# Attention scores of two heads on half of the array's rows each, in place of zero padded keys

## The chip, the cores and the metric

One core of a Trainium2 chip runs the whole program. Its engines are TensorE (PE; its weight loads are listed apart as PEld), VectorE (DVE), ScalarE (ACT), GpSimd (POOL) and SyncE (SP), each with its own instruction stream that it works through in order. The metric is device time in microseconds (us), median of the runs.

## What is computed

The program is two blocks after each other. The change touches the first one, an attention block on 512 tokens of width 1024 with two kinds of heads of 64 channels. In "A", eight query heads share two heads of keys and values, look back over a window of 128 positions and have a sink in the softmax. In "B", eight heads have keys and values of their own and a mask with three dilations. Cut to what matters here:

```
q_a, k_a = rope(rmsnorm(q_a)), rope(rmsnorm(k_a))       # 8 and 2 heads of 64
o_a = softmax with sink(q_a k_a^T / 8 + window mask) v_a
q_b, k_b = rope(rmsnorm(q_b)), rope(rmsnorm(k_b))       # 8 and 8 heads of 64
o_b = dilated softmax(q_b k_b^T / 8) v_b
x = x + concat(o_a * silu(g_a), o_b * silu(g_b)) @ w_out
```

A second block follows (two layers with a convolution, a state space scan and 16 experts); its code is the same before and after.

## The kernel before

The tokens are four blocks of 128. Projections (line 271, function `mm3`) split each fp32 operand in a high and a low part and add three products in PSUM. Queries and keys come out with the token on the partition, `head_norm_rope` (lines 455 to 469) norms and rotates them, and `transposed` (line 538) turns the heads of a pair into a tile with 128 rows: 64 channels of one head above 64 of the other. `qT` is such a tile of queries. For the keys there are four tiles `kz[i][j]`: `i` says in which half of the rows a head's keys stand (the other half is zeros, written once by GpSimd on line 532), `j` alternates between key heads (A) or pairs (B). With the zeros, `qT` with both heads against `kz[n][j]` gives the scores of head n alone, from a matmul over all 128 rows.

`attend` handles one head: four blocks of queries, each with a score matmul (line 552) of `nb * 128` columns into a PSUM bank `ax` (there are three banks of that name), and a DVE instruction that adds the mask, writes the scores to `P` in SBUF and gives the negative of each row's maximum, `negm` (line 555). In A, `nb` is 1, 2, 2, 2; in B, 1, 2, 3, 4. Then come the exponentials with their sums on ACT (line 564), the reciprocal (568) and four scalings on DVE (570). `values` turns the scaled P back with transposes (line 581, also into `ax`), copies them (584 on ACT, 586 on DVE) and multiplies by v (line 589), the two heads of the pair in two halves of the array's columns. There are four pairs in A and four in B.

Nothing in the code fixes how the engines' streams are interleaved: a scheduler orders the instructions of all of block 1 when the program is built. It fills the time of a softmax on TensorE with projections of later stages (line 271), and it mixes on DVE the softmax with splits of weights (256), with `head_norm_rope` of the next stage's queries and keys, and with gates. In `head_norm_rope` DVE makes `hxn` (463), GpSimd reads it in two instructions (466), DVE then overwrites `hxn` (468), which must wait until GpSimd has read it, and adds (469).

## Time and profile before

| | us |
|---|---|
| median of 3 runs (1655.51 to 1656.25) | 1655.83 |
| span of the profiled execution, first to last instruction | 1652.9 |
| PE busy, share of the span | 1431.6 (87%) |
| DVE busy | 1107.1 (67%) |
| ACT busy | 774.2 (47%) |
| POOL busy | 327.0 (20%) |
| mean granted TensorE clock | 0.933 |

The profiled execution's own time isn't listed beside its span; the median lies 2.9 us above the span. The scores stand between 72.8 and 246.9 us, in the first seventh of the program. A timeline row gives the start, the length, the engine, the line and operation, the output and inputs, how many instructions were merged, and in brackets the idle time of the engine before it with what ended it. Each fp32 score matmul leaves two records, as it runs in two parts.

### The profile page before, as it was taken

Reading aid. Unit: us, or ns where it says so; the run is one execution under the profiler, and the core shown is the slowest. Engines: PE = TensorE matmul, PEld = TensorE weight load, DVE = VectorE, ACT = ScalarE, POOL = GpSimd, SP = SyncE. Lnnn points to the kernel's source line nnn. Section 1 sums busy time; section 2 is a strip of 40 time slices with the busy share of each in tenths; the row PEclk is TensorE's granted clock in tenths of the full one; section 3 lists DMA queues with packets and bytes.
Section 4 is the critical chain, followed back from the end, with each engine's and each line's share of the span. In section 5 each row is a group of like instructions: output and inputs, shape, how many; then the busy total and the mean of one; then the engine's idle time right before and its main releaser. Section 6 shows DMA issues by size and latency. Waiting matters only on the chain. (4 is left out here: it accounts for less than half of the span.)

```text
span 1652.9 us, 21781 instructions
## 1 busy us (share of the span) xinstructions
PE 1431.6 (87%) x7746; PEld 1062.8 (64%) x7754; DVE 1107.1 (67%) x2318; ACT 774.2 (47%) x1367; POOL 327.0 (20%) x259
## 2 busy tenths in 40 slices
PE   7989999979999898996776997589999897977882
PEld 5878767858888553664555776268874365755661
DVE  5877555459999655525975675479966455789772
ACT  5444555234532455423554565335425443666651
POOL 1212000000000320001533343000013001359641
PEclk9999999979999999999897999689999899899896
DMA  5111244121213177424787896511215753799853
GB/s 212 52 52 57 77 153 141 64 90 51 64 62 130 60 243 245 140 74 162 242 268 239 244 265 171 186 42 61 77 64 176 232 194 140 239 322 318 296 165 125
DMA packets 74835, 256.07 MB, mean 155 GB/s; under 512 B 10080, under 2 KB 12512, under 8 KB 74592
## 3 DMA queue, kind: packets, MB, share of 16 engines
q1 hardware_dynamic: 64640, 225.77, 39.9%
q0 software_dynamic: 10080, 28.86, 7.3%
q8 instruction: 62, 1.02, 0.3%
q14 instruction: 53, 0.43, 0.1%
HBM read 230.46 MB, written 31.98 MB: 159 GB/s over the span
## 5 line engine op out<-in xcount | busy, mean ns | idle before, releaser
L271 PE MATMUL mm<-act,uhi 128*128 128x512 f32 (+1 forms) x1504 | 324.0, 362 | 4.4 <-ACT act L416 4.1
L271 PEld LDWEIGHTS mm<-act,uhi 128*128 128x128 f32 x1504 | 249.6, 193 | 68.5 <-issue 16.0
L271 PE MATMUL mm<-act,ulo 128*128 128x512 f32 (+1 forms) x752 | 167.7, 358 | 0.0
L271 PEld LDWEIGHTS mm<-act,ulo 128*128 128x128 f32 x752 | 125.8, 193 | 24.3 <-issue 4.6
L255 ACT ACTIVATE uhi<-raw 128x1024 fp32r<-128x1024 f32 x58 | 61.2, 1059 | 112.0 <-PE mm L271 84.2
L806 DVE SCALAR_TENSOR_TENSOR cvx<-vx,pr,cvx 128x456 f32<-128x456 f32 (+18 forms) x176 | 107.8, 616 | 2.3 <-ACT cvx L789 1.2
L1407 PE MATMUL mm<-act,uhi 128*128 128x512 f32 x328 | 96.6, 417 | 14.2 <-ACT uhi L255 14.2
L271 PE MATMUL mm<-whi,act 128*128 128x256 f32 x576 | 84.4, 293 | 10.7 <-ACT whi L255 10.5
L382 PE MATMUL ad<-raw,sc 128*32 128x512 f32 x384 | 87.9, 658 | 4.9 <-DMA raw<-wada 2.8
L1445 POOL DMA_INDIRECT acc<-k,idx x35 | 67.3, 1923 | 117.0 <-ACT k L1442 35.0
L256 DVE TENSOR_TENSOR ulo<-raw,uhi 128x1024 fp32r<-128x1024 f32 x58 | 70.7, 1221 | 24.5 <-ACT uhi L255 9.1
L271 PEld LDWEIGHTS mm<-whi,act 128*128 128x128 f32 x576 | 76.4, 197 | 14.2 <-ACT whi L255 10.5
L256 DVE TENSOR_TENSOR act<-rawm,act 128x1024 fp32r<-128x1024 f32 x52 | 68.2, 1312 | 20.0 <-ACT act L255 17.4
L256 DVE TENSOR_TENSOR part<-rawm,part 128x1024 fp32r<-128x1024 f32 x40 | 57.0, 1427 | 35.4 <-ACT part L255 27.3
L1407 PEld LDWEIGHTS mm<-act,uhi 128*128 128x128 f32 x328 | 61.7, 196 | 27.7 <-ACT uhi L255 15.1
L1394 PE MATMUL ax<-cs,k 128*128 128x128 f32 x280 | 42.4, 298 | 38.0 <-DMA k<-t_d,idx 38.0
L256 DVE TENSOR_TENSOR act<-raw,act 128x1024 fp32r<-128x1024 f32 x51 | 67.3, 1322 | 11.8 <-ACT act L255 11.5
L990 POOL TENSOR_TENSOR xw<-xstc,swgtc 128x512 f32<-128x512 f32 x8 | 9.7, 1232 | 313.8 <-ACT xstc L844 177.0
L1407 PE MATMUL mm<-part,uhi 128*128 128x512 f32 x232 | 67.5, 412 | 3.6 <-ACT uhi L255 3.2
L271 PE MATMUL mm<-act,whi 128*128 128x512 f32 x256 | 69.9, 412 | 0.0
L255 ACT ACTIVATE act<-rawm 128x1024 fp32r<-128x1024 f32 x52 | 55.1, 1059 | 25.7 <-PE mm L1407 16.7
L255 ACT ACTIVATE act<-raw 128x1024 fp32r<-128x1024 f32 x60 | 63.0, 1053 | 8.2 <-DMA raw<-wd 3.7
(497 smaller groups left out, 3058.1 us busy)
## 6 DMA issues: line engine op xcount, KB each, us to landing
raw<-wada SPq DMA_DIRECT2D x96, 512.0 KB, 5.0
raw<-wgu SPq DMA_DIRECT2D x66, 512.0 KB, 6.3
rawm<-wgu SPq DMA_DIRECT2D x62, 512.0 KB, 6.3
raw<-win SPq DMA_DIRECT2D x40, 512.0 KB, 3.7
raw<-wd SPq DMA_DIRECT2D x34, 512.0 KB, 6.1
rawm<-wd SPq DMA_DIRECT2D x30, 512.0 KB, 6.6
raw<-w SPq DMA_DIRECT2D x26, 512.0 KB, 5.2
raw<-wo SPq DMA_DIRECT2D x24, 512.0 KB, 4.8
```

The lines of the kernel that those rows point to most:

```text
L255: self.nc.scalar.activation(hi, raw, AF.Copy)
L256: (eng or self.nc.vector).tensor_sub(lo, raw, hi.bitcast(F32))
L271: nc.tensor.matmul(out, lhsT=(ah, ah, al)[p], rhs=(bh, bl, bh)[p], start=(start and p == 0 and i == 0), stop=(stop and p == 2 and i == n - 1))
L382: nc.tensor.matmul(ps[32 * g:32 * g + 32], lhsT=self.sc[:, 4 * h + g, :], rhs=w[g // 2][:, 512 * (g % 2):512 * (g % 2) + 512], start=(h == ...
L806: nc.vector.scalar_tensor_tensor(o_, v_, cw[:, l, i, k:k + 1], o_, op0=OP.mult, op1=OP.add)
L990: nc.gpsimd.tensor_tensor(hv(xw), hv(s.xst[:, c]), s.wgt[:, c, 8 * d:8 * d + 8, None].to_broadcast([128, 8, 64]), op=OP.mult)
L1394: nc.tensor.transpose(pt[:, 128 * k:128 * k + 128], j.xg[:, 512 * hf + 128 * k:512 * hf + 128 * k + 128], self.ident)
L1407: nc.tensor.matmul(pg, lhsT=(xh, xl, xh)[p][:, 4 * q + k, :], rhs=(wh, wh, wl)[p][k // 2][:, 512 * (k % 2):512 * (k % 2) + 512], start=(n ...
L1445: nc.gpsimd.indirect_dma_start(out=acc[:, :], out_offset=bass.IndirectOffsetOnAxis(ap=j.sid, axis=0), in_=y, in_offset=None, bounds_check= ...
```

## The change

The keys of a pair stand in one tile `kk[j]` of 128 rows, one head in each half, with no zeros. A score matmul takes 64 rows of `qT` and the same 64 rows of `kk`, so head 0 uses the upper half of the array's rows and head 1 the lower half. `attend` now handles a pair: for each block of queries it issues the matmuls of both heads into two `ax` banks and then the two DVE instructions. The softmax of both heads (`softmax`, the same instructions as before) follows when all eight score matmuls of the pair are written in the code. In B the keys of a pair are copied by one instruction of 128 rows instead of two of 64; the four memsets of GpSimd go. The diff also drops comments and the unused constant's branch (`SCP`), which change nothing.

```
-            kz = [[self.tile(pool, f"kz{i}{j}", [128, 512], bufs=1) for j in range(2)] for i in range(2)]
-            for i in range(2):
-                for j in range(2):
-                    nc.gpsimd.memset(kz[i][j][64 * (1 - i):64 * (1 - i) + 64], 0.0)
...
+            kk = [self.tile(pool, f"kk{j}", [128, 512], bufs=1) for j in range(2)]
...
-            def attend(which, h, qT, kT, mask, span):
...
+            def attend(which, pair, qT, kT, mask, span):
...
-                    sc = (self.mm if SCP[which] else self.ax)(nb * 128)
-                    nc.tensor.matmul(sc, lhsT=qT[:, 128 * j:128 * j + 128],
-                                     rhs=kT[:, 128 * (j + 1 - nb):128 * (j + 1)], start=True, stop=True)
...
+                    scs = [self.ax(nb * 128) for _ in range(2)]
+                    for n, sc in enumerate(scs):
+                        nc.tensor.matmul(sc, lhsT=qT[64 * n:64 * n + 64, 128 * j:128 * j + 128],
...
+                    for (h, negm, lsum, P, tiles), sc in zip(heads, scs):
+                        p = tiles[place[j][0]][:, place[j][1]:place[j][1] + nb * 128]
...
-                for i in range(2):
-                    nc.vector.tensor_copy(kz[i][p % 2][64 * i:64 * i + 64], pt[64 * i:64 * i + 64])
+                nc.vector.tensor_copy(kk[p % 2], pt)
...
-                Ps = [attend(1, 2 * p + n, qT, kz[n][p % 2], self.C("maskB"), 4) for n in range(2)]
+                Ps = attend(1, p, qT, kk[p % 2], self.C("maskB"), 4)
```

The scheduler makes a new order of block 1 from this. Behind the block all engines' orders are as before. Two places show what moves. The first is TensorE at the first pair of B; L552 and L551 are the score matmuls, L271 projections, L581 and L585 the transposes of P, in which the number behind the name tells which of the pair's tiles it is. Before:

```order
L552 MATMUL ax_2037<-kz_11_117,qT_2017 128x128
L552 MATMUL ax_2040<-kz_11_117,qT_2017 128x256
L552 MATMUL ax_2043<-kz_11_117,qT_2017 128x384
L552 MATMUL ax_2046<-kz_11_117,qT_2017 128x512
L552 MATMUL ax_2063<-kz_13_119,qT_2017 128x128
L552 MATMUL ax_2066<-kz_13_119,qT_2017 128x256
L271 MATMUL mm_2160<-act_97,whi_2149 128x512
L552 MATMUL ax_2069<-kz_13_119,qT_2017 128x384
L552 MATMUL ax_2072<-kz_13_119,qT_2017 128x512
L271 MATMUL mm_2160<-act_97,whi_2149 128x512
L271 MATMUL mm_2160<-act_99,whi_2149 128x512
L581 MATMUL ax_2084<-cs,P_2034 128x128
```

The same place after:

```order
L551 MATMUL ax_2035<-kk_11_117,qT_2011 128x128
L551 MATMUL ax_2036<-kk_11_117,qT_2011 128x128
L551 MATMUL ax_2041<-kk_11_117,qT_2011 128x256
L551 MATMUL ax_2042<-kk_11_117,qT_2011 128x256
L551 MATMUL ax_2047<-kk_11_117,qT_2011 128x384
L551 MATMUL ax_2048<-kk_11_117,qT_2011 128x384
L551 MATMUL ax_2053<-kk_11_117,qT_2011 128x512
L551 MATMUL ax_2054<-kk_11_117,qT_2011 128x512
L271 MATMUL mm_2153<-act_97,whi_2142 128x512 x2
L271 MATMUL mm_2153<-act_99,whi_2142 128x512 x2
L271 MATMUL mm_2153<-act_94,whi_2142 128x512 x2
L585 MATMUL ax_2077<-cs,P_2027 128x128
```

The eight scores now alternate between the heads and stand in one piece, and six projections stand between them and the first transpose, where four stood around and behind the scores.

The second place is DVE at the fourth pair of A, between the scores' instructions and the first scaling of P. L567 and L571 add the sink to the sums, L568 and L572 are the reciprocals, L570 and L574 the scalings; L463, L468 and L469 are `head_norm_rope` of B's keys, the other rows its rsqrt. Before:

```order
L567 TENSOR_TENSOR lsum_1037<-lsum_1037,es_1052 128x4
L323 TENSOR_SCALAR rsg_1634<-rsg_1634 128x16
L568 RECIPROCAL lsum_1037<-lsum_1037 128x4
L324 TENSOR_SCALAR rsm_1632<-rsm_1632 128x16
L327 TENSOR_TENSOR rsq_1633<-rsg_1634 128x16
L570 TENSOR_SCALAR P_1038<-P_1038,lsum_1037 128x128
```

The same place after:

```order
L330 SCALAR_TENSOR_TENSOR hr_1618<-rsq_1627,hr_1618 128x16
L463 TENSOR_TENSOR hxn_1642<-b_233_1160,hr_1618 128x512
L463 TENSOR_TENSOR hxn_1648<-b_233_1160,hr_1618 128x512
L468 TENSOR_TENSOR hxn_1642<-hxn_1642,tC_1474 128x512
L571 TENSOR_TENSOR lsum_1031<-lsum_1031,es_1062 128x4
L468 TENSOR_TENSOR hxn_1648<-hxn_1648,tC_1474 128x512
L572 RECIPROCAL lsum_1031<-lsum_1031 128x4
L469 TENSOR_TENSOR b_233_1160<-hxn_1642,b_233_1160 128x4x128
L574 TENSOR_SCALAR P_1032<-P_1032,lsum_1031 128x128
```

Two `hxn`, both of their overwritings and one addition have moved ahead of the reciprocal and the scaling. Of the four pairs of A, the first and the third had the two L463, one or two L468 ahead of the first scaling before as well; after, the first, third and fourth have the rows shown here, with L469. On TensorE the projections of 256 columns between a pair's first score and its first transpose number 47, 29, 32 and 25 before, and 58, 30, 41 and 47 after.

## Rows read from the trace of the kernel before

**Rows 1.** Busy time by stretch: TensorE, its weight loads, DVE, ACT, POOL, clock, DMA.

```profile
core 0: us, PE busy (x) PEld busy (x) DVE busy (x) ACT busy (x) POOL busy (x), PEclk, DMA share, GB/s
60.00:335.00 275.00, 266.79 (x1646) 206.75 (x1645) 168.50 (x486) 126.53 (x283) 19.82 (x23) 0.98 0.26 87
```

**Rows 2.** Timeline of TensorE, third pair of A: scores, projections, first transpose.

```profile
110.85 3.44 PE L552 MATMUL ax<-kz,qT 128*128 128x128 f32 x16
113.94 0.70 PE L271 MATMUL mm<-wlo,act 128*128 128x256 f32 x3
...
120.52 0.48 PE L581 MATMUL ax<-cs,P 128*128 128x128 f32 x1 [2.46 <-DVE P L570]
```

**Rows 3.** Timeline of TensorE around the first pair of B.

```profile
174.19 1.11 PE L271 MATMUL mm<-whi,act 128*128 128x256 f32 x8
175.13 1.04 PE L538 MATMUL ax<-cs,b 128*128 128x128 f32 x8
...
177.03 3.12 PE L552 MATMUL ax<-kz,qT 128*128 128x128 f32 x12
179.80 0.59 PE L271 MATMUL mm<-act,whi 128*128 128x512 f32 x1
180.29 1.77 PE L552 MATMUL ax<-kz,qT 128*128 128x384 f32 x4
181.50 1.04 PE L271 MATMUL mm<-act,whi 128*128 128x512 f32 x2
```

**Rows 4.** Timeline of DVE, reading the scores of that pair.

```profile
177.64 0.29 DVE L555 CUSTOM_DVE_ANT_0 P<-ax,cs 128x128 f32<-128x128 f32 x1
...
180.15 0.28 DVE L555 CUSTOM_DVE_ANT_0 P<-ax,cs 128x128 f32<-128x128 f32 x1
...
180.37 0.42 DVE L555 CUSTOM_DVE_ANT_0 P<-ax,cs 128x256 f32<-128x256 f32 x1
180.71 0.08 DVE L555 DVE_READ_ACCUMULATOR2_ANT negm<- 128x1 f32 x1
```

**Rows 5.** Timeline of TensorE, first pair of A: its stall, later values and transposes.

```profile
84.52 0.33 PE L581 MATMUL ax<-cs,P 128*128 128x128 f32 x1 [2.67 <-DVE P L570]
...
89.98 0.66 PE L589 MATMUL op<-PT,kva 128*64 128x128 f32 x8
90.57 0.66 PE L581 MATMUL ax<-cs,P 128*128 128x128 f32 x4
```

**Rows 6.** Timeline of DVE, third pair of A: norm and rope ahead of the scaling.

```profile
115.14 1.29 DVE L463 TENSOR_TENSOR hxn<-b,hr 128x512 f32<-128x512 f32 x2
...
117.77 1.20 DVE L468 TENSOR_TENSOR hxn<-hxn,tC 128x512 f32<-128x512 f32 x1 [0.71 <-POOL b L466]
...
119.58 0.69 DVE L468 TENSOR_TENSOR hxn<-hxn,tC 128x512 f32<-128x512 f32 x1 [0.52 <-POOL b L466]
120.19 1.06 DVE L570 TENSOR_SCALAR P<-P,lsum 128x128 f32<-128x128 f32 x4
...
121.53 0.66 DVE L469 TENSOR_TENSOR b<-hxn,b 128x512 f32<-128x512 f32 x1
```

**Rows 7.** Timeline of POOL beside the softmax of A's first pair.

```profile
80.76 3.61 POOL L466 TENSOR_TENSOR b<-hxn,tS 128x256 f32<-128x256 f32 x4 [10.99 <-DVE lsum L567]
```

**Rows 8.** Timelines, fourth pair of A: scores and first transpose on TensorE.

```profile
131.60 2.48 PE L552 MATMUL ax<-kz,qT 128*128 128x128 f32 x12
...
137.83 0.33 PE L581 MATMUL ax<-cs,P 128*128 128x128 f32 x1
```

**Rows 9.** Timeline of DVE, fourth pair of A: first read of scores, later rows.

```profile
132.02 0.29 DVE L555 CUSTOM_DVE_ANT_0 P<-ax,cs 128x128 f32<-128x128 f32 x1 [1.69 <-PE ax L552]
...
135.83 0.69 DVE L351 TENSOR_TENSOR P<-cs,xr 128x512 f32<-128x512 f32 x1
...
137.50 1.06 DVE L570 TENSOR_SCALAR P<-P,lsum 128x128 f32<-128x128 f32 x4
```

**Rows 10.** Busy time and clock behind the third pair's stall, and in B.

```profile
120.20:127.00 6.80, 6.48 (x27) 5.27 (x27) 4.39 (x16) 0.65 (x2) 0.00 (x0) 0.51 0.00 0
180.00:330.00 150.00, 149.74 (x809) 105.73 (x808) 81.27 (x200) 72.31 (x145) 0.24 (x1) 1.00 0.34 113
```

**Rows 11.** Line 675, the copies of B's keys: count, shortest, median and longest in ns.

```profile
L675 DVE COPY kz<-ax x8: 681/688/695, 176.2 to 240.5; 64x512 f32<-64x512 f32 x8
```

More of the change, by code (lines that the diff above doesn't have):

```diff
@@ L539, in transposed @@
                 return pt
-            def attend(which, h, qT, kT, mask, span):
+            def attend(which, pair, qT, kT, mask, span):
                 W = span * 128
-                negm = self.tile(self.sm, "negm", [128, 4])
-                lsum = self.tile(self.sm, "lsum", [128, 4])
-                P = []
-                tiles = [PT() for _ in range(2 + which)]
+                heads = []
+                for n in range(2):
+                    negm = self.tile(self.sm, "negm", [128, 4])
+                    lsum = self.tile(self.sm, "lsum", [128, 4])
+                    heads.append((2 * pair + n, negm, lsum, [], [PT() for _ in range(2 + which)]))
                 place = ((0, 0), (0, 256), (1, 0), (1, 256)) if which == 0 else ((0, 0), (1, 0), (0, 128), (2, 0))
@@ L550, in attend, with softmax @@
                     nb = min(j + 1, span)
-                    sc = (self.mm if SCP[which] else self.ax)(nb * 128)
-                    nc.tensor.matmul(sc, lhsT=qT[:, 128 * j:128 * j + 128],
-                                     rhs=kT[:, 128 * (j + 1 - nb):128 * (j + 1)], start=True, stop=True)
-                    p = tiles[place[j][0]][:, place[j][1]:place[j][1] + nb * 128]
-                    nc.vector.tensor_tensor_reduce(p, sc, mask[:, W - nb * 128:W], -1.0, 1e30, OP.add, OP.min,
-                                                   negm[:, j:j + 1])
-                    P.append(p)
+                    scs = [self.ax(nb * 128) for _ in range(2)]
+                    for n, sc in enumerate(scs):
+                        nc.tensor.matmul(sc, lhsT=qT[64 * n:64 * n + 64, 128 * j:128 * j + 128],
+                                         rhs=kT[64 * n:64 * n + 64, 128 * (j + 1 - nb):128 * (j + 1)],
+                                         start=True, stop=True)
+                    for (h, negm, lsum, P, tiles), sc in zip(heads, scs):
+                        p = tiles[place[j][0]][:, place[j][1]:place[j][1] + nb * 128]
+                        nc.vector.tensor_tensor_reduce(p, sc, mask[:, W - nb * 128:W], -1.0, 1e30, OP.add, OP.min,
+                                                       negm[:, j:j + 1])
+                        P.append(p)
+                return [softmax(which, h, negm, lsum, P) for h, negm, lsum, P, _ in heads]
+            def softmax(which, h, negm, lsum, P):
                 if which == 0:
@@ L638, in block1 @@
                 for i in range(2):
-                    nc.vector.tensor_copy(kz[i][(i + kv) % 2][64 * i:64 * i + 64], pt[64 * i:64 * i + 64])
+                    nc.vector.tensor_copy(kk[(i + kv) % 2][64 * i:64 * i + 64], pt[64 * i:64 * i + 64])
             for p in range(4):
@@ L643, in block1 @@
                 opair, kv = self.op(), p // 2
-                Ps = [attend(0, 2 * p + n, qT, kz[n][kv], self.C("maskA"), 2) for n in range(2)]
+                Ps = attend(0, p, qT, kk[kv], self.C("maskA"), 2)
                 values(Ps, lambda i: [kva[:, i, 192 + 64 * kv:192 + 64 * kv + 64]] * 2, 2, opair)
```

## The prediction

> **What bounds the kernel now.** First I read the busy times by stretch: from 60 to 335 us, where all scores lie, TensorE is busy 266.8 of 275 us and DVE 168.5 [rows 1]. So TensorE sets the pace of this part, and a microsecond taken from its stream counts in full if no wait takes its place. Then I read its timeline for the gaps. Two large ones lie in A, both ended by DVE's scaling of P: 2.67 us at the first pair [rows 5] and 2.46 us at the third [rows 2]. At the fourth pair the first transpose starts at 137.83, 0.33 us behind the scaling, and without a gap [rows 8, 9]. In B there is none: 149.74 us busy of 150, at full clock [rows 10]. Third, the price of the scores. A pair of A takes TensorE from 110.85 to 113.94, 3.09 us [rows 2]; a pair of B 2.77 and 1.21 us with one projection between, 3.98 us [rows 3]. Four pairs of each are 4 x 3.09 + 4 x 3.98 = 28.3 us, 1.7% of the time.
>
> **Scores on half of the rows.** If the two heads ran wholly side by side, half of that, 14.1 us, would go. What limits this is who empties the banks. Three banks serve eight scores, so the fourth score of a pair waits for the first read by DVE, and the eighth for the fifth. DVE's reads follow each other after 0.22 us for 128 columns and 0.34 us for 256 [rows 4], so 0.46 and 0.58 for 384 and 512 at the same step. A pair of B thus needs 2 x (0.22 + 0.34 + 0.46 + 0.58) = 3.2 us of DVE, hardly less than the 3.98 us that TensorE needs today; the two are near balance already.
>
> The twelve records of 1664 columns (128, 256, 384, 512, 128, 256) took 2.77 us [rows 3], 1.66 ns a column: 0.21 us for 128, 0.64 for 384, 0.85 for 512. The first read starts 0.61 us behind the first score [rows 3, 4], 0.40 behind the end of its columns. The chain of the second, fifth and eighth score in B: second read done at 0.61 + 0.22 + 0.22 = 1.05; fifth score until 1.69, its read from 2.09 to 2.55; eighth score until 3.40. The least, by the sum of reads alone, is 0.61 + 1.58 + 0.85 = 3.04.
>
> Going over to half rows and back is not in this trace for rows, but it is for columns. Eight records of 128 columns of the values' product take 0.59 us, 89.98 to 90.57 [rows 5]. One after another they would take 8 x 0.106 = 0.85, two at a time 0.42; so halves do run together, and a visit costs 0.17 more. I take 0.15 a visit for row halves as well. A pair of B then takes 3.2 to 3.55 us instead of 3.98. I take 0.5 us saved, near the chain, 2.0 us in four pairs.
>
> In A the same chain with a first read after 0.42 us [rows 8, 9] gives 0.42 + 0.44 + 0.43 + 0.40 + 0.34 + 0.43 + 0.15 = 2.6 instead of 3.09. Norm rows stand among DVE's reads there, so I take 0.3 a pair, 1.2 us. Together **-3.2 us**, bounds -1 and -5.5.
>
> **What DVE does ahead of the scaling.** The softmax of head 0 now waits for both heads' reads, and the scheduler put more of the next stage's norm and rotation ahead of P's scaling. Everything queued behind it on DVE waits, and TensorE, in order, waits at the first transpose. The third pair shows the price: from the first `hxn` at 115.14 to the scaling at 120.19 DVE needs 5.05 us, of which little is its own work: both overwritings wait for GpSimd [rows 6]. The addition that has moved ahead as well costs 0.66 us [rows 6].
>
> First pair: GpSimd ends its four instructions at 80.76 + 3.61 = 84.37 [rows 7]. Behind that come the second overwriting (0.69), the addition (0.66), the small reciprocal (0.2) and 0.33 us to the transpose: 86.25 in place of 84.52, 1.73 later. Eleven more projections fill 11 x 0.1175 = 1.3 us (eight take 0.94 [rows 3]). With scores 0.3 shorter, the stall is 2.67 + 1.73 - 1.3 + 0.3 = 3.4 us. Third pair: 2.46 + 0.66 - 9 x 0.1175 + 0.3 = 2.4. Both together, 5.8 in place of 5.1: **+0.7 us**.
>
> Fourth pair: no stall before; the scaling came 5.9 us behind the first score [rows 8, 9]. After, the two `hxn`, GpSimd's four instructions, both overwritings and an addition come first. Reads and L351 end 4.9 us behind the first score today (135.83 + 0.69 - 131.60 [rows 8, 9]); I keep 5.0 for them and the rest of the rsqrt. Then 5.05 + 0.66 + 0.33 gives the first transpose at 11.0. TensorE is there after 2.8 + 47 x 0.1175 = 8.3. **+2.7 us**, between 0 (if the projections last longer) and 4.
>
> Behind the third pair's stall the clock stood at 0.51 for 6.8 us [rows 10], which is the lower of its two levels, 1.2 GHz. Dense work would lose half of that, 3.3 us. A third stall of this size should bring one more such stretch, and part of the values' work there waits anyway: **+2.4 us**, between 0 and 3.4.
>
> **At no cost.** Eight copies of 0.69 us [rows 11] become four that I expect to be as long each, 2.8 us less on DVE; in B it is TensorE that is full [rows 10], so nothing is gained. The four memsets leave GpSimd's stream ahead of any score. If B's transposes must wait for the later softmax, up to the 2.0 us saved there is given back; two more projections at the first pair are there to fill it, so I take nothing, and keep it for the range. Behind block 1 the orders are the same; the rest only shifts.
>
> **The sum.** -3.2 + 0.7 + 2.7 + 2.4 = +2.6 us against the profiled execution, whose span of 1652.9 lies 2.9 under the median: 1655.8 + 2.6 = **1658.4 us**.
>
> **The rivals.**
> 1. The waits are hidden: the fill of 47 and 58 projections covers DVE's longer queue, no further cold stretch comes, and the scores' 3.2 us remain: 1652.6. For it speaks that the scheduler gave most projections to just these pairs; against it that it left 2.67 and 2.46 us where the same rows stood ahead.
> 2. The halves don't run together, so the change doesn't do what it says: each score takes 1.66 ns a column alone, the 3.2 us are not saved, and eight visits at 0.15 add 1.2: 1658.4 + 4.4 = 1662.8, slower. It decides from the point where a pair's two scores start one behind the other's end. The values' column halves speak against it [rows 5].
> 3. The scores really halve: -14.1 us and nothing given back: 1641.7. It needs DVE to read twice as fast as it does or more banks; the reads' pace speaks against it [rows 4].
> 4. Half used rows let the clock fall at every pair of B and A: eight stretches of 3.4 us (half of the one in [rows 10]) at half speed cost 13.6 us: 1672. B's column halves stand in 150 us at 1.00 [rows 10], which speaks against it.
>
> The Trainium skill, "TensorEngine Tiling (Array Packing)", section Theoretical Speedup, gives up to two times for a contraction of 64 or less. By that rule alone the time would be that of rival 3; the trace agrees with it for columns (0.59 in place of 0.85 us) and has no row tile to show it for rows.
>
> **How the numbers follow.** The forecast has 0.66, rival 1 0.17, rival 2 0.09, rival 3 0.03, rival 4 0.05. A measurement of this kernel can tell about 0.2%, 3.3 us, from no change. The forecast at +2.6 lies just inside; its unknown terms (scores -5.5 to -1, fourth pair 0 to 4, clock 0 to 3.4, B's transposes 0 to 2) put 0.30 of its 0.66 above +3.3 and 0.36 within. Rival 1 gives 0.11 to no change and 0.06 to faster. Slower: 0.30 + 0.09 + 0.05 = 0.44; same: 0.36 + 0.11 = 0.47; faster: 0.06 + 0.03 = 0.09. The range reaches from rival 1 with slightly more saved, 1652, past rival 2, 1664; rivals 3 and 4 and the tails stay out.
>
> **What would show it.** Score records of a pair in pairs that start within some ns of each other, and a pair of B's scores in 3.2 to 3.6 us: right on the halves. Gaps of TensorE ended by the scaling of P at the first, third and fourth pair of A, near 3.4, 2.4 and 2.7 us, each followed by clock near 0.5: right on DVE's order. Wrong if the fourth pair has no gap, if gaps appear inside the blocks of scores, or if the clock in B falls under 1.00. Block 1's end, some 335 us in, should move by as much as the whole.

## The result, and the profile after

The changed kernel took 1667.55 us (median of 10 runs, 1662.1 to 1672.4) beside 1655.67 for the kernel before on the same chip: by the medians 11.9 us slower, a ratio of 1.0072. The ratio on record, given with its interval, is a little smaller, 1.0062 (95%: 1.0042 to 1.0081). On two other chips the same two kernels gave 1.0066 and 1.0069 on record. The prediction had slower by 2.6 us, 1658.4, and a range that ended at 1664.

The page of the changed kernel, its span and its busy times:

```profile
span 1666.9 us, 21782 instructions
...
PE 1440.2 (86%) x7746; PEld 1062.1 (64%) x7754; DVE 1101.2 (66%) x2314; ACT 774.5 (46%) x1367; POOL 322.4 (19%) x255
```

The stretch that answers to [rows 1], with the same columns:

```profile
60.00:335.00 275.00, 261.55 (x1616) 198.53 (x1615) 164.18 (x482) 124.32 (x280) 17.91 (x20) 0.97 0.26 87
```

TensorE is busy 261.6 us of 275 where it was busy 266.8. It issues the same 2000 records up to L342 (below), waits more, and ends them later. I follow three marks in both traces: the start of L342, which ends block 1 on TensorE; the first projection (L271) behind it; and the end.

| profiled execution, us | before | after | more |
|---|---|---|---|
| start of L342 | 335.6 | 343.0 | 7.4 |
| from there to the first L271 | 18.8 | 22.5 | 3.7 |
| from there to the end of the span | 1298.5 | 1301.4 | 2.9 |

The first two make 11.1 of the 11.9 us by which the medians differ. The third is less than what two executions of one program differ by in that part (further down), so nothing is read into it. The first moves from execution to execution as well: three profiles with TensorE's order of before have L342 at 335.2 to 337.9, five with the changed order have it at 339.9 to 344.5.

**The blocks of scores.** TensorE and then DVE (every other kind of read left out) at the first pair of B, which answers to [rows 3] and [rows 4]:

```profile
181.19 3.76 PE L551 MATMUL ax<-kk,qT 64*128 64x128 f32 x16
184.89 1.43 PE L271 MATMUL mm<-act,whi 128*128 128x512 f32 x5
```

```profile
181.70 0.29 DVE L556 CUSTOM_DVE_ANT_0 P<-ax,cs 128x128 f32<-128x128 f32 x1 [0.66 <-PE ax L551]
...
182.79 0.42 DVE L556 CUSTOM_DVE_ANT_0 P<-ax,cs 128x256 f32<-128x256 f32 x1 [0.22 <-PE ax L551]
...
184.44 0.69 DVE L556 CUSTOM_DVE_ANT_0 P<-ax,cs 128x512 f32<-128x512 f32 x1 [0.18 <-PE ax L551]
```

The block holds TensorE from 181.19 to 184.89, 3.70 us in place of 3.98. The first two scores start 6 ns apart. No later pair does: the two of 256 columns start 0.55 us apart, those of 384 0.36, those of 512 0.56, since from the fourth score on each waits until DVE has emptied a bank. Then DVE waits for them (0.22 and 0.18 us in the rows). A pass of 512 columns here takes 0.53 us to the next on its half. Taken as the time from each score record to TensorE's next record, the eight blocks of the program take 28.1 us after and 27.4 before; only the first pair of A and the first two of B are shorter, by 0.1 to 0.3.

This measure is too kind to full rows. Behind their last pass the projection's record starts 0.03 us later, while the pass still runs; it lasts 0.80 us, the next one 0.40. The same place before:

```profile
181.47 0.59 PE L552 MATMUL ax<-kz,qT 128*128 128x512 f32 x1
181.50 0.80 PE L271 MATMUL mm<-act,whi 128*128 128x512 f32 x1
182.14 0.40 PE L271 MATMUL mm<-act,whi 128*128 128x512 f32 x1
```

With half rows the next record starts 0.52 us behind the last pass. From a pair's first score to the next pair's, with the same instructions on TensorE in between, the first two pairs of B take 21.70 and 19.69 us before, 21.15 and 18.77 after: 0.55 and 0.92 less. For the other pairs the projections in between differ; there only a measure over the whole block compares (below).

**The stalls of A.** The three first transposes that waited for P's scaling (first and third pair, then the fourth with its scores), beside [rows 5], [rows 2] and [rows 8]:

```profile
86.24 0.33 PE L585 MATMUL ax<-cs,P 128*128 128x128 f32 x1 [2.97 <-DVE P L574]
```

```profile
123.49 0.33 PE L585 MATMUL ax<-cs,P 128*128 128x128 f32 x1 [2.39 <-DVE P L574]
```

```profile
133.45 3.22 PE L551 MATMUL ax<-kk,qT 64*128 64x128 f32 x16
...
144.70 0.42 PE L585 MATMUL ax<-cs,P 128*128 128x128 f32 x1 [2.30 <-DVE P L574]
```

They are 0.3 longer, 0.1 shorter and 2.3 new. Behind the third and the new one the clock (the number ahead of the last two) is 0.75 over 6.8 us: half of each stretch at 1.2 GHz, half at 2.4. Before, the third pair had 0.51 over the whole 6.8 [rows 10].

```profile
123.50:130.30 6.80, 6.80 (x41) 5.41 (x41) 4.20 (x15) 2.60 (x6) 0.00 (x0) 0.75 0.00 0
144.70:151.50 6.80, 6.80 (x38) 5.52 (x40) 4.80 (x14) 2.44 (x4) 0.00 (x0) 0.75 0.00 0
```

**New waits behind B's last pair.** TensorE:

```profile
260.73 1.09 PE L593 MATMUL op<-PT,b 128*64 128x128 f32 x14
261.75 1.92 PE L382 MATMUL ad<-raw,sc 128*32 128x512 f32 x16
264.93 1.05 PE L388 MATMUL ad<-cs,P 128*128 128x2 f32 x8 [1.26 <-ACT P L385]
265.92 1.07 PE L302 MATMUL ax<-P,cs 128*32 128x256 f32 x6
268.08 2.50 PE L271 MATMUL mm<-act,whi 128*128 128x512 f32 x5 [1.10 <-ACT whi L255]
```

The last adaLN step of block 1 (L382, L388) now stands alone behind the values, without a projection in its pauses. With another wait of 0.27 that ends at 228.83 this makes 2.6 us, where B had none [rows 10].

**The join of block 1 and the next part.** TensorE again:

```profile
342.97 1.05 PE L342 MATMUL ax<-cs,P 128*128 128x1 f32 x8 [0.69 <-ACT P L305]
347.25 2.08 PE L355 MATMUL ax<-P,cs 128*128 128x512 f32 x2 [3.22 <-DVE P L351]
358.82 3.64 PE L382 MATMUL ad<-raw,sc 128*32 128x512 f32 x16 [9.50 <-DVE P L415]
363.27 1.87 PE L388 MATMUL ad<-cs,xw 128*128 128x2 f32 x8 [0.80 <-ACT xw L385]
365.48 0.79 PE L271 MATMUL mm<-act,uhi 128*128 128x256 f32 x2 [0.34 <-ACT uhi L255]
```

Before, L382 ran right behind L355, from 341.84 on, and the long wait (7.17 us) stood behind it at L388. After, L382 itself waits for the last of the L415, where DVE reads the norm's factor that L355 wrote. The order of instructions is the same; the bank is not. The factor is a tile `ax` of block 1 and lies in bank 0, and bank 0 is `ad` in the next part, by the banks that the two programs assign. In the kernel before, the rotation of the three `ax` banks had put it in bank 2. No trace shows these numbers; that the bank is the cause is tested below (e1_join).

**The 7.4 us up to L342.** TensorE has 2000 records up to there in both programs:

```profile
0.00:335.55 335.55, 315.63 (x2000) 249.50 (x2000) 207.43 (x616) 156.61 (x331) 29.01 (x40) 0.98 0.30 100
0.00:342.96 342.96, 317.44 (x2000) 244.85 (x2000) 203.66 (x612) 155.87 (x331) 26.99 (x36) 0.98 0.29 97
```

Its waits (idle times over 0.1 us) add up to 19.7 us before and 25.5 after. Of the 5.8 more, 0.25 lie in the first 60 us, 0.30 - 0.07 + 2.30 at the stalls, 2.63 in B, and 0.36 inside the third block of B, where scores wait for a bank. The stretches at 1.2 GHz add up to 13.6 and 17.1 us; work that fills them loses half, 1.7 more. What is left, TensorE's own time for its 2000 records, is 309.1 before and 309.0 after. So the change as a whole took nothing off it. (In ten other profiles with three `ax` banks this own time is 308.2 to 311.6.)

### The profile page after: what moved, and what is told of

It reads as the page before. It is cut to its first block, busy times and chain, and to the rows that moved or that the text cites. A ratio compares the mean times of both kernels' runs of the same rounds, so it can differ in the third digit from the quotient of the medians.

```text
span 1666.9 us, 21782 instructions
## 1 busy us (share of the span) xinstructions
PE 1440.2 (86%) x7746; PEld 1062.1 (64%) x7754; DVE 1101.2 (66%) x2314; ACT 774.5 (46%) x1367; POOL 322.4 (19%) x255
## 5 line engine op out<-in xcount | busy, mean ns | idle before, releaser
L271 PE MATMUL mm<-act,uhi 128*128 128x512 f32 (+1 forms) x1504 | 322.4, 360 | 4.4 <-ACT act L416 3.9
L271 PEld LDWEIGHTS mm<-act,uhi 128*128 128x128 f32 x1504 | 248.0, 192 | 68.5 <-issue 16.0
L271 PE MATMUL mm<-act,ulo 128*128 128x512 f32 (+1 forms) x752 | 166.6, 356 | 0.0
L271 PEld LDWEIGHTS mm<-act,ulo 128*128 128x128 f32 x752 | 124.3, 191 | 24.6 <-issue 4.6
L382 PE MATMUL ad<-raw,sc 128*32 128x512 f32 x384 | 89.6, 673 | 13.5 <-DVE P L415 9.5
L271 PE MATMUL mm<-whi,act 128*128 128x256 f32 x576 | 86.0, 297 | 11.0 <-ACT whi L255 10.8
L271 PEld LDWEIGHTS mm<-whi,act 128*128 128x128 f32 x576 | 77.6, 201 | 16.3 <-ACT whi L255 10.8
L256 DVE TENSOR_TENSOR ulo<-raw,uhi 128x1024 fp32r<-128x1024 f32 x58 | 70.7, 1221 | 23.5 <-PE mm L271 13.8
L256 DVE TENSOR_TENSOR act<-rawm,act 128x1024 fp32r<-128x1024 f32 x52 | 69.3, 1332 | 22.5 <-ACT act L255 19.8
L256 DVE TENSOR_TENSOR part<-rawm,part 128x1024 fp32r<-128x1024 f32 x40 | 54.0, 1352 | 38.7 <-ACT part L255 29.3
L256 DVE TENSOR_TENSOR act<-raw,act 128x1024 fp32r<-128x1024 f32 x51 | 66.9, 1314 | 11.8 <-ACT act L255 11.4
L271 PE MATMUL mm<-act,whi 128*128 128x512 f32 x256 | 68.4, 409 | 1.1 <-ACT whi L255 1.1
L255 ACT ACTIVATE act<-rawm 128x1024 fp32r<-128x1024 f32 x52 | 55.0, 1058 | 28.6 <-PE mm L1410 19.7
```

The source lines that it names most:

```text
L255: self.nc.scalar.activation(hi, raw, AF.Copy)
L256: (eng or self.nc.vector).tensor_sub(lo, raw, hi.bitcast(F32))
L271: nc.tensor.matmul(out, lhsT=(ah, ah, al)[p], rhs=(bh, bl, bh)[p], start=(start and p == 0 and i == 0), stop=(stop and p == 2 and i == n - 1))
L382: nc.tensor.matmul(ps[32 * g:32 * g + 32], lhsT=self.sc[:, 4 * h + g, :], rhs=w[g // 2][:, 512 * (g % 2):512 * (g % 2) + 512], start=(h == ...
```

## The experiments

A table of all of them stands at the end of this section. Ratios are to the kernel before on the same chip, as the record gives them; they are not quite the quotients of the two medians. "Own" is TensorE's own time up to L342: without its waits, and without half of the stretches at 1.2 GHz.

### What a half of the rows can do: e4_probe

```
+        def run(rows, N, count):
+            for i in range(count):
+                r = rows[i % len(rows)]
+                b = out[i % 4 + (4 if r == (64, 128) else 0)]
+                nc.tensor.matmul(b[:, :N], lhsT=h[r[0]:r[1], 128 * (i % 4):128 * (i % 4) + 128],
+                                 rhs=h[r[0]:r[1], :N], start=True, stop=True)
```

> The kernel before, with matmuls in fp32 behind its end whose results nobody reads, in banks of their own, so that no bank and no reader holds them up: 64 with all rows and 512 columns; then 16 on the upper half alone, 16 full, 16 on both halves in turn, 16 full; the same with 128 columns (32 each), with 256 in turn and full, and last 32 of 256 columns full and upper half in turn. Each is two passes. Theory (a pass on a half pays its own weight load): 512 columns on one half 0.53 us a pass against 0.43 full; in turn 0.27; 128 columns 0.21 on one half against 0.107 full, in turn 0.107, so that nothing is gained at 128 columns and 1.3 at 256. Rival (halves overlap fully): one half as full, in turn half of it, 0.21 and 0.053 a pass. Third: going between full and half rows costs extra, by what the last piece takes over the mean of the two.

Busy times by stretch, one stretch a sequence: 16 of 512 columns on one half, full, on both halves in turn; then 32 of 128 columns in the same three ways; last 32 of 256 full, and full and half in turn.

```profile
1698.15:1712.08 13.93, 13.93 (x34) 5.91 (x33) 0.00 (x0) 0.00 (x0) 0.00 (x0) 1.00 0.01 1
1712.08:1726.01 13.93, 13.93 (x34) 6.00 (x33) 0.00 (x0) 0.00 (x0) 0.00 (x0) 1.00 0.00 0
1726.01:1733.08 7.07, 7.07 (x34) 3.02 (x33) 0.00 (x0) 0.00 (x0) 0.00 (x0) 1.00 0.00 0
...
1747.01:1754.35 7.34, 7.34 (x66) 7.22 (x65) 0.00 (x0) 0.00 (x0) 0.00 (x0) 1.00 0.01 2
1754.35:1761.69 7.34, 7.34 (x66) 7.22 (x65) 0.00 (x0) 0.00 (x0) 0.00 (x0) 1.00 0.00 0
1761.69:1765.46 3.77, 3.77 (x66) 3.65 (x65) 0.00 (x0) 0.00 (x0) 0.00 (x0) 1.00 0.02 4
...
1779.91:1793.83 13.92, 13.92 (x67) 12.27 (x66) 0.00 (x0) 0.00 (x0) 0.00 (x0) 1.00 0.00 0
1793.83:1813.87 20.04, 20.04 (x65) 9.35 (x63) 0.00 (x0) 0.00 (x0) 0.00 (x0) 1.00 0.00 1
```

With banks to spare, two halves in turn take half the time (7.07 against 13.93, 3.77 against 7.34), and one half alone takes what full rows take. My theory of a weight load in every pass falls. What costs is going between full and half rows: the last pass of one kind takes 0.52 us to the next record and the first of the other 0.53, all others 0.43. So 32 matmuls in turn take 20.04 in place of 13.92 us, 0.19 each. In the changed kernel a score behind a wait begins with 0.53, too. The probe has no waits in it, but full rows behind one do the same: some 1448 us into the kernel before, a first projection pass behind a wait of 0.74 us takes 0.34 us to the next, the second 0.24.

### The order by pairs without half rows: e2_full_rows

```
-                        nc.tensor.matmul(sc, lhsT=qT[64 * n:64 * n + 64, 128 * j:128 * j + 128],
-                                         rhs=kT[64 * n:64 * n + 64, 128 * (j + 1 - nb):128 * (j + 1)],
+                        nc.tensor.matmul(sc, lhsT=qT[:, 128 * j:128 * j + 128],
+                                         rhs=kT[n][:, 128 * (j + 1 - nb):128 * (j + 1)],
```

> The same as the run on the join, but with the zero padded keys of the kernel before and all 128 rows in each score matmul: only the order by pairs and the softmax behind all eight scores are kept of the change. DVE's stream in A is that of the changed kernel. Theory 2 (half rows give nothing here, the order is what costs): a pair of B takes 3.9 to 4.1 us of TensorE against 3.7, a pair of A 3.0 to 3.2 against 3.1; the stalls of pairs 1, 3 and 4 of A stay near 3.0, 2.4 and 2.3; time within 2 us of the run on the join, 1664. Rival (half rows cost time by themselves, by weight loads or the clock): 3 us or more faster than the run on the join, 1661 or less. Rival (half rows did save the 3.2 us forecast, and something else took it): 3 us slower, 1667.

By the records the blocks of scores take 28.1 us, as with half rows; TensorE's own time is 309.0 us with either; L342 starts at 342.2 (343.0 in the changed kernel, 341.1 and 339.9 in the two profiles with the join's edit), and the first transposes wait 8.2 us in four waits:

```profile
PE ax L588 <- DVE P L577: 8.2, 4, 3.0
```

So in the trace half rows gave nothing in this order, and the stalls belong to the order. By pair, from first score to first score without waits, half rows took 0.4 to 0.6 us less in the first, second and fourth pair of B, 1.1 more in the third, and 0.5 more in A's four together. The time, 1664.3, lies within the 2 us of what I expected, 1664; it is 4.7 us under e1_join, measured beside it, where the theory said 2 at most, with intervals that overlap.

### Half rows without the order by pairs: e3_half_by_head

```
+                    rw = slice(64 * (h % 2), 64 * (h % 2) + 64)
+                    nc.tensor.matmul(sc, lhsT=qT[rw, 128 * j:128 * j + 128],
+                                     rhs=kT[rw, 128 * (j + 1 - nb):128 * (j + 1)], start=True, stop=True)
```

> The kernel before with half rows alone: keys of a pair in one tile, score matmuls over 64 rows, but head after head, each with its softmax, as before the change (and L355's factor in op). DVE's and TensorE's order in A is that of the kernel before. If two passes on the same half follow each other only after the weight load, as the changed kernel's records suggest (0.53 us from pass to pass for 512 columns where full rows took 0.43), each of a pair's 16 passes costs 0.1 more: a pair of B 5.6 us in place of 3.98, one of A 4.6 in place of 3.09; eight pairs up to 13 us, time 1665 to 1669. If not, a pair takes what it took before and the time is that of the kernel before, 1655.7. The stalls of A: pair 4 has none, pairs 1 and 3 keep 2.7 and 2.5 or shrink where the scores last longer.

1671.0 us, slower still, and 2 us above the range expected (before took 2.3 us more on this chip than on the first). A pair of B holds TensorE 4.5 to 4.8 us:

```profile
180.46 2.91 PE L550 MATMUL ax<-kk,qT 64*128 64x128 f32 x12
183.30 0.49 PE L271 MATMUL mm<-act,whi 128*128 128x512 f32 x1
183.72 1.77 PE L550 MATMUL ax<-kk,qT 64*128 64x384 f32 x4
```

By the records that is 0.6 to 1.0 more than with full rows; from first score to first score it is 22.00 and 19.84 us at the first two pairs of B, 0.30 and 0.15 more than before. Both are less than the 1.6 expected, in keeping with the probe: passes of one half that follow each other cost nothing more, beginnings and changes do. TensorE's own time is some 2.5 us more in all. The rest up to L342 is 2.3 us of waits and twice as much time at 1.2 GHz (27.3 us in place of 13.6). In A the blocks take 3.4 to 3.6 us; the first, 6.14 us, lay in a cold stretch (1.2 GHz) that began at 71.9 us behind a wait and lasted 13.7 us; whether half rows kept it cold stays open, from one profile:

```profile
73.10:79.50 6.40, 6.40 (x20) 4.88 (x20) 2.99 (x15) 4.07 (x11) 0.00 (x0) 0.50 0.00 0
```

### More banks: e5_four_banks, e8_before_four_banks, e9_four_and_three

The first two take the fourth `ax` bank from the projections (`PB = (2, 4)`), in the changed kernel and in the kernel before. The third takes it from the adaLN products of block 1:

```
-PB = (3, 3)
+PB = (3, 4)
...
-            ps = self.psum("ad", 1)
+            ps = self.ad(512)
...
+            self.ad = self.ax
```

> The changed kernel with four ax banks and two mm banks (three and three before), and L355's factor in op. In the run with probes, halves with banks to spare run fully side by side (0.214 us a pass of 512 columns in place of 0.429), and each fresh start after a pause costs 0.1. Theory (the three banks held the halves back): the second pair of scores now starts at once, a pair of B takes 2.9 us against 3.7, one of A 2.3 against 3.1, sum of the eight 21 to 22 us against 28.1; pair 4 of A has no norm rows ahead of its scaling in this order, so its stall of 2.3 us goes too; block 1 ends 6 to 8 us earlier than in the changed kernel. Rival (DVE's reads set the length of the scores, 3.2 us for a pair of B and some 2.2 for A): the sum falls by 2 us or less, the stall's 2.3 remain the whole gain. Rival (two mm banks are too few): waits of projections (L271) on ACT or DVE appear and take the gain back.

> The kernel before, full rows and head by head, with four ax and two mm banks (and L355's factor in op): what the banks alone are worth. Theory (the banks matter for halves that can overlap, hardly for full rows, which TensorE works through one after another): the sum of the score blocks stays 25.5 to 27.5 us, time within 2 us of before, more if two mm banks are too few. Rival (the banks alone bring the gain): the time falls by as much as four banks bring the changed kernel.

> The changed kernel with four ax banks and still three mm banks: in block 1 the adaLN products (L382, L388) use ax and give up their own bank (and L355's factor goes to op). DVE's order in A is that of the changed kernel, so the stalls of pairs 1, 3 and 4 stay. Theory (banks are what held the halves back; two mm banks cost some 6 us of block 1 both for full and for half rows): the score blocks take 23 us in all as in the run with four and two, the waits of projections near 107, 260 and 297 us of that run go, and L342 comes 4 to 6 us earlier than in the changed kernel, near 337 to 339. Time 1668.5 - 3.7 (the join) - 5 = 1660. Rival (projections run out in B as in the changed kernel, so that TensorE waits later for what it did earlier): the score blocks shrink to 23 us but L342 stays within 2 us of 342.8.

The same pair of B as above, with four and three banks:

```profile
180.18 2.91 PE L552 MATMUL ax<-kk,qT 64*128 64x128 f32 x16
183.01 1.66 PE L271 MATMUL mm<-act,whi 128*128 128x512 f32 x6
```

```profile
181.48 0.42 DVE L557 CUSTOM_DVE_ANT_0 P<-ax,cs 128x256 f32<-128x256 f32 x1
...
182.48 0.55 DVE L557 CUSTOM_DVE_ANT_0 P<-ax,cs 128x384 f32<-128x384 f32 x1
...
182.96 0.69 DVE L557 CUSTOM_DVE_ANT_0 P<-ax,cs 128x512 f32<-128x512 f32 x1
```

2.83 us in place of 3.70, and DVE no longer waits ahead of the second read of 256 columns or the first of 512. All blocks together: 23.1 us (four and two; 1 us more than expected) and 22.7 (four and three) in place of 28.1. With full rows the same bank is worth nothing: 27.6 against 27.4. TensorE's own time says it more fully: half rows 309.0 with three banks and 299.9 with four (303.8 where the projections have only two), full rows 309.1 with three, 308.8 with four and two for projections, and 308.3 with four and three (e15_all_full_rows, below). That settles why nothing was saved: the banks, not the halves and not DVE's pace by itself. The Trainium skill, "TensorEngine Tiling (Array Packing)", section PSUM Bottleneck, says that tiling speeds up TensorE and not the emptying of PSUM; these runs agree, by 5 to 9 us of TensorE's own time for a fourth bank. Its section Restrictions and Gotchas says that different row tiles write to different banks; every score here has a bank of its own, so no run tests that.

Two banks for projections are too few: L342 starts at 341.8 with full rows (335.6 with three), and TensorE's waits show it. In e5_four_banks (waited for, us in all, times, longest):

```profile
PE mm L271 <- DVE hT L701: 2.4, 1, 2.4
...
PE mm L271 <- ACT whi L255: 1.2, 1, 1.2
```

In e8_before_four_banks the same two are 2.4 and 1.9 us (the second, 1.1 us long, stands in the changed kernel as well). In e5_four_banks the fourth pair's stall shrinks to 0.4 us, as expected, and L342 comes 5.3 us earlier than in the changed kernel, not 6 to 8. With three again (e9_four_and_three) neither wait is there, L342 starts at 334.9, 8 us earlier than in the changed kernel, and the time is 1658.6, as expected to within 1.4 us. The stalls of A stay, 10.6 us with B's smaller ones:

```profile
PE ax L586 <- DVE P L575: 10.6, 7, 2.8
```

### The bank at the join: e1_join, e13_join_again, with e7 and e14

```
-            self.xhd = self.modnorm([self.hT[:, k, :] for k in range(8)], S, 0, 0, PT)
+            self.xhd = self.modnorm([self.hT[:, k, :] for k in range(8)], S, 0, 0, PT, bank=self.op)
```

> The changed kernel, with one edit: the factor of block 1's last norm (L355) is written into the bank named op and not into ax. In the changed kernel this factor lies in the bank that the next part's first adaLN product (L382) takes; in the kernel before it lay in another, so there L382 did not wait for DVE's last reads (L415). Theory 1 (a bank that met by accident): TensorE has no wait of 9.5 us ahead of L382; L382 starts right behind L355, the wait of some 7.2 us stands behind it at L388 as before the change, and L388 comes 3.7 us earlier. Block 1 up to L342 stays as it is (L342's wait ends near 343). Time 1667.6 - 3.7 = 1663.9, ratio to before 1.005. Rival (the adaLN weights themselves land late, or ACT is what L388 waits for in any case): L382 starts earlier and L388 does not, time 1667.6, ratio 1.007.

> The changed kernel with L355's factor in op, once more, beside the changed kernel on the same chip. Theory (the wait for the bank is 3.7 us of the whole time): L382 right behind L355, L342 to the first projection behind it 18.8 us against 22.5, and a median 2 to 5 us under that of the changed kernel. Rival (what the join gives is taken back further on): medians within 1.5 us of each other.

> The changed kernel as it is, as the measure for the others on the same chip. 11 to 12 us over the kernel before; in its profile block 1's end (L342) some 7.4 us later than before, the wait of 9.5 us ahead of L382, the score blocks 28.1 us in all.

> The changed kernel as it is, beside the others of this call: 1.006 to 1.007 of before, the score blocks 28.1 us, 22.5 us from L342 to the first projection behind it.

TensorE in e13_join_again:

```profile
339.85 1.05 PE L342 MATMUL ax<-cs,P 128*128 128x1 f32 x8 [0.69 <-ACT P L305]
344.13 2.08 PE L355 MATMUL op<-P,cs 128*128 128x512 f32 x2 [3.23 <-DVE P L351]
346.13 3.64 PE L382 MATMUL ad<-raw,sc 128*32 128x512 f32 x16
356.95 1.86 PE L388 MATMUL ad<-cs,xw 128*128 128x2 f32 x8 [7.17 <-ACT xw L385]
358.67 1.63 PE L271 MATMUL mm<-act,uhi 128*128 128x256 f32 x6
```

L382 stands right behind L355 again, and from L342 to the first L271 it is 18.8 us, as before the change. The 3.7 us in the trace, and the bank as their cause, are shown. That they reach the whole time is not: the first of these runs was expected at 1663.9 and took 1669.0; the second took 1665.6 beside 1669.5 for the changed kernel on one chip, 4.0 us that are no more than what two programs of one order differ by (e11_before_op, below).

The two profiles show one thing more. TensorE's order and the three stalls (7.7 us) are those of the changed kernel, but the stretches at 1.2 GHz up to L342 add up to 6.8 us in each, not 17.1, with none behind the fourth pair's stall, and L342 starts at 341.1 and 339.9.

### DVE's order in A: e6_rope_behind, e12_rope_again, e11_before_op

```
-            nc.vector.tensor_tensor(xn, xn, at(tC, i), op=OP.mult)
-            nc.vector.tensor_tensor(h64(out), xn, h64(out), op=OP.add)
+            with self.tc.issue_after(behind) if behind is not None else ExitStack():
+                nc.vector.tensor_tensor(xn, xn, at(tC, i), op=OP.mult)
+                nc.vector.tensor_tensor(h64(out), xn, h64(out), op=OP.add)
```

> The kernel before, full rows and head by head, with one edit of DVE's order: the overwriting and the addition of head_norm_rope (L468, L469) for the first three of B's four groups are issued behind the last scaling of P of pairs 1, 3 and 4 of A. Theory (these waits for GpSimd ahead of the scaling are what stalls TensorE in A): the gaps of 2.67 and 2.46 us at the first transposes of pairs 1 and 3 go, and with them the cold stretches behind them; block 1 ends 5 to 8 us earlier, time 5 to 8 us under the kernel before. Rival (TensorE then waits elsewhere, because B's keys come later or the projections run out): the gaps return elsewhere and the time is within 2 us of before.

> The kernel before with L468 and L469 behind the scaling of P, once more. Its block 1 was 6.6 us shorter in the profile and its time the same as before; behind block 1 the profile showed a cold stretch of 17 us from 630 us on that the profile of before did not have. Theory (that stretch comes and goes from execution to execution, as with the probes' run of the kernel before): the profile's part behind block 1 lies anywhere from 1298 to 1309 us, and the median of all runs of this kernel together falls to 3 to 6 us under before. Rival (the part behind block 1 is longer whenever it starts at this point): 1309 us again, time within 2 us of before.

> The kernel before with L355's factor in op and nothing else. All engines' orders are those of the kernel before, and the bank was free before as well: time 0 us from before, as a check on how far two programs with the same order differ, and on the part from block 1's end on: 1303 us by the medians, 1298.5 in the profile of before, 1309 in those of the runs on the join and on the rope.

The stalls go: 0.8 us at the first transposes in two waits (e6_rope_behind) where the kernel before had 5.1.

```profile
PE ax L586 <- DVE P L573: 0.8, 2, 0.6
```

L342 starts at 329.0 and 332.8 in the two profiles, 335.6 before, but the times are 1.0008 and 0.9995 of before. One place where it went is seen in the first profile: a part where TensorE waits in small pieces, some 640 us in, ran cold that had run nearly at full speed before. 20 us from about the same instruction on, before (93 records on TensorE) and in e6_rope_behind (69):

```profile
635.00:655.00 20.00, 16.95 (x93) 7.04 (x94) 11.65 (x42) 9.12 (x17) 0.00 (x0) 0.94 0.82 281
```

```profile
630.00:650.00 20.00, 17.67 (x69) 7.31 (x68) 8.89 (x32) 8.00 (x15) 0.00 (x0) 0.59 0.48 157
```

That comes by itself, too: in e4_probe, which is the kernel before up to there, this part took 6.6 us more than in the profile of before. But in the second profile (e12_rope_again) the clock there was 0.83, and the part behind block 1 took 1303.5 us, not 1309 as in the first. So the rival's time came true without its reason, the theory's chance did not bring the median down, and where this gain goes stays open. The gain itself is 3 to 7 us by L342, which lay 3.8 us apart in these two profiles of one program.

e11_before_op, with all orders as in the kernel before, gave 1660.0 against 1655.7, interval 0.9995 to 1.0042. So two programs that do the same can differ by 4 us in medians of 12 and 35 runs, and I read nothing from a difference below that by itself.

### All together, and what half rows are worth in it: e10_all, e16_all_again, e15_all_full_rows

> The run with four ax and three mm banks, with the end of head_norm_rope (L468, L469) for three of B's groups issued behind the scaling of P of pairs 1, 3 and 4 of A as well: half rows with all that the other runs took out of their way. Theory: score blocks 23 us, no stall over 1 us at the first transposes of A, L342 near 326 to 330 us against 335.6 before and 329.0 with full rows and the same order of DVE. If half rows are worth anything once the rest is out of the way, L342 comes before 328; if the projections that fill the softmax run out, it does not, and waits of TensorE stand behind 255 us. The time of the whole follows block 1 only if the part behind it (some 1303 us by the medians) stays.

> Half rows with four ax and three mm banks, L468 and L469 behind the scaling, L355's factor in op, once more: 0.996 of before, score blocks 23.6 us, L342 near 326, no stall over 1 us at A's first transposes.

> The kernel before, full rows and head by head, with the three other edits of the best version: four ax and three mm banks, L468 and L469 behind the scaling, L355's factor in op. Theory (half rows with banks to spare are worth their 4 to 5 us of TensorE): score blocks 27.5 to 28 us, L342 some 3 us later than in e16, time 1653 to 1656, 4 us over e16. Rival (banks and DVE's order alone make the best version): 1649 as e16, L342 at 326.

Half rows, four and three banks, DVE's order and the join's edit: 1649.0 and 1647.7 us, 0.9960 (0.9941 to 0.9978) and 0.9933 (0.9909 to 0.9957) of before. Of A's stalls this is left (e10_all, waits of TensorE, then the first pair):

```profile
PE ax L591 <- DVE P L578: 4.0, 6, 0.8
```

```profile
82.38 0.33 PE L591 MATMUL ax<-cs,P 128*128 128x128 f32 x1 [0.74 <-DVE P L578]
```

With full rows and the same three edits: 1652.9, 0.9985 (0.9963 to 1.0007). Beside it on one chip half rows took 5.3 us less, one comparison and not far above the 4.3 us of e11_before_op. In the trace TensorE's own time up to L342 is 7.4 us less (300.9 against 308.3; by the score records 4.4). Its waits are 4.1 us longer (23.3 against 19.2), most of them at the first transposes, 4.0 against 0.6, and L342 starts 3.4 us earlier. So once the rest is out of its way the change takes 7 us off TensorE's work, and some 3 to 5 are left of them.

| us | score blocks | own | L342 | to the first L271 | median | before | ratio |
|---|---|---|---|---|---|---|---|
| before | 27.4 | 309.1 | 335.6 | 18.8 | | | |
| changed | 28.1 | 309.0 | 343.0 | 22.5 | 1667.6 | 1655.7 | 1.0062 |
| e7_after_again | 28.1 | 309.1 | 342.8 | 22.6 | 1668.5 | 1656.3 | 1.0066 |
| e14_after_third | 28.2 | 308.5 | 344.5 | 23.1 | 1669.5 | 1656.6 | 1.0069 |
| e1_join | 28.2 | 310.4 | 341.1 | 18.8 | 1669.0 | 1658.0 | 1.0067 |
| e13_join_again | 28.1 | 309.9 | 339.9 | 18.8 | 1665.6 | 1656.6 | 1.0053 |
| e2_full_rows | 28.1 | 309.0 | 342.2 | 19.2 | 1664.3 | 1658.0 | 1.0040 |
| e3_half_by_head | 35.3 | 311.6 | 347.2 | 18.6 | 1671.0 | 1658.0 | 1.0075 |
| e5_four_banks | 23.1 | 303.8 | 337.7 | 18.8 | 1660.6 | 1656.3 | 1.0030 |
| e8_before_four_banks | 27.6 | 308.8 | 341.8 | 18.8 | 1663.5 | 1656.3 | 1.0029 |
| e9_four_and_three | 22.7 | 299.9 | 334.9 | 18.8 | 1658.6 | 1655.7 | 1.0022 |
| e11_before_op | 27.7 | 308.2 | 337.9 | 18.8 | 1660.0 | 1655.7 | 1.0019 |
| e6_rope_behind | 27.9 | 310.6 | 329.0 | 18.8 | 1657.0 | 1656.3 | 1.0008 |
| e12_rope_again | 27.9 | 310.5 | 332.8 | 18.8 | 1655.5 | 1655.7 | 0.9995 |
| e15_all_full_rows | 28.0 | 308.3 | 329.2 | 18.8 | 1652.9 | 1656.6 | 0.9985 |
| e10_all | 23.6 | 300.9 | 326.2 | 18.8 | 1649.0 | 1655.7 | 0.9960 |
| e16_all_again | 23.6 | 300.9 | 325.9 | 18.8 | 1647.7 | 1656.6 | 0.9933 |

## Why the prediction was wrong

It had the sign, and missed the size by 9.3 us. By its own steps:

- **Scores on half of the rows, -3.2: wrong, +0.3.** TensorE's own time did not fall (309.0 against 309.1), and 0.36 us of waits for a bank came inside the third block of B, the gaps that the prediction had named as a sign that it was wrong. Beside full rows in the same order (e2_full_rows) three pairs of B saved 0.4 to 0.6 us each, where 0.5 was forecast; the third took 1.1 more, as a split of weights (L256, 1.23 us) stood among DVE's reads; and A, forecast at -1.2, took 0.5 more. In the fourth pair of A three small rsqrt instructions stand among DVE's first five reads, which are done 2.39 us behind the first score, forecast 2.03. I wrote that three banks set the limit and still took a saving in all eight pairs; e9_four_and_three shows that with a fourth TensorE's own time falls by 9 us.
- **What came right in it, in part by luck.** Three pairs of B saved what was forecast, but not by its steps. The chain held up to the fifth score's read (ahead of it 2.02 us, forecast 2.09; done at 2.50, forecast 2.55), but the last score took 1.05, not its rate of 0.85, since it begins behind a wait and the next instruction goes back to full rows, at 0.1 each; and the block before is longer than the 3.98 that I read, as its last pass runs on under the next record. Nor were two prices right: a visit to half rows, taken at 0.15, costs 0.38 in the probe, and the price of A's blocks before was that of the longest of the four (3.09; the others 2.80 to 2.98).
- **Stalls, +0.7 and +2.7: right.** 3.0, 2.4 and 2.3 us where 3.4, 2.4 and 2.7 were forecast, 2.5 more in all.
- **One more cold stretch, +2.4: not shown.** In the profile of the result the number came: the new stall has one behind it, the third pair's became shorter, and another stands at the waits behind B; in all 3.4 us more at 1.2 GHz, which costs 1.7 at most. But the stretches vary within one order: 6.8 us in all in e1_join and e13_join_again, with the same three stalls and none of it behind the fourth pair's, and 17.1 in e11_before_op, with the order of before and no fourth stall.
- **"At no cost": wrong, +2.6.** I took B's transposes as covered by the projections that moved ahead of them. They are, and TensorE waits 2.6 us behind B's last pair instead. That the moved projections are what is missing there is argued, not shown: e9_four_and_three, where no fewer stand ahead, waits there 0.73 us, and once more as long at 216 us.
- **"Behind block 1 the orders are the same; the rest only shifts": wrong, +3.7.** The orders are the same and the waits are not. The next part's first product met a bank that was still being read (e1_join); that a change in block 1 turned the rotation of its banks is read from the programs, not from a trace.
- **The bound of 0.2%.** The runs tell less: the medians of two programs of one order differed by 4.3 us (e11_before_op).

3.5 for the scores, 2.6, 3.7 and 0.25 from the start, less 1.6 by which stalls and clock were forecast too high, make 8.5 of the 9.3 us. L342 moved by 7.4 us, where the prediction had it move by as much as the whole.

Of the rivals, the second (halves that don't run together) came nearest with 1662.8, but for another reason: behind the first two scores of a pair the two of a block do start one behind the other, and it is not the halves, which the probe shows side by side, but the banks. The rate of the third, for which the prediction cited the Trainium skill's Theoretical Speedup ("TensorEngine Tiling (Array Packing)"), is reached in the probe (7.07 against 13.93 us) and nowhere in this kernel. The fourth did not come: from 180 to 260 us the clock stayed at 1.00. Only the one cold stretch over A's first scores in e3_half_by_head leaves it a doubt.

## What to carry to other kernels

Halving the work of an engine saves nothing while its results wait for buffers: count the buffers along the chain, and give the new overlap its bank before you count the gain. An edit that only seems to shift what follows can change which bank or buffer meets which; look at the waits of the first instructions behind the changed part, not only at their order. To price such a change, compare stretches with the same instructions on both sides: by the records of the changed line alone half rows saved 4.4 us in the last comparison, by TensorE's own time 7.4. The change alone cost 12 us; with three small edits around it 7 to 9 are gained, of which full rows with the same edits have some 4.

## What the runs showed of the hardware

In the probe two row halves with banks of their own run wholly side by side in fp32: 0.214 us a pass of 512 columns, 0.429 full, and one half alone gains nothing. Each change between full and half rows costs 0.19 us, 0.09 on the last pass of the one kind and 0.10 on the first of the other (626 ns a matmul of 256 columns in turn, 435 full). A first pass behind a wait takes 0.1 us longer as well (0.34 in place of 0.24 for full rows some 1448 us in). The clock of a part in which TensorE waits in small pieces is not the same in every execution of one program: some 640 us in, that was worth 6.6 us between two profiles of the same instructions.
